# Measured durations as the interleaver's prices, streams that wait until an engine should be done, a chunked convolution and sums issued by need, in a streaming encoder layer on one core

## The chip, the cores and the metric

The kernel runs on one core of a Trainium2 chip. The metric is device time in microseconds (us) of one execution. TensorE (PE) multiplies matrices, VectorE (DVE), ScalarE (ACT) and GpSimd (POOL) work on tiles of 128 partitions, SyncE (SP) and POOL issue DMA transfers. Each engine takes its instructions in the order in which the program lists them for that engine, and an instruction waits on semaphores for what it reads or overwrites.

## The reference

One inference step of one layer on 512 prompt tokens and 8 sequences of 16 sample tokens (640 tokens, 1024 channels). Three branches come out of one projection, are gated and summed, and a feed-forward part follows. All in float32.

```python
z = x @ w_in                                   # 1024 -> 6656
xa, ya, glu, q, gates = split(z)
h = rg_lru(causal_depthwise_conv(xa, width 4))  # associative scan over positions
out_a = (h * gelu(ya)) @ proj_a
u = glu[..., :512] * sigmoid(glu[..., 512:])
v = causal_depthwise_conv(concat(history 30, u), width 31)
out_b = silu(layer_norm(v)) @ proj_b
out_c = mem_cross_attention(q, k, v) @ proj_c   # 4 heads, 256 memory tokens
g = sigmoid(gates + b_gate)
merged = g0 * out_a + g1 * out_b + g2 * out_c
x = layer_norm(alpha * x + merged @ w_out)
x = layer_norm(alpha * x + (silu(x @ w_ffn_gate) * (x @ w_ffn_up)) @ w_ffn_down)
```

The outputs are x for both groups and the new states of the two convolutions, of the recurrence and of the memory's keys and values.

## The kernel before

**Precision and tiles.** A float32 matrix is written as a high and a low part in the matmul's fp32r type; a product takes three matmuls (high by high, high by low, low by high). The activations lie with channels on partitions and the 640 tokens along the free dimension, as `xh` and `xl` (eight blocks of 128 channels). A matmul takes a 128x128 weight block and 320 tokens. ACT copies a weight tile to its high part (`wh`), DVE, and for some steps POOL, subtracts it from the float32 tile to get the low part (`wl`). Other tiles come from a pool of 52 slots of 128x640 (`Slots`, L110), handed out in the order in which they were freed; `s` with a number is such a slot.

**The list of steps.** `Step` (L268) is one weight tile with its matmuls. The list holds, in order: the memory's keys and values, the GLU halves and the queries, the recurrence's input `xa`, the gate of branch c and `proj_c`, gate and `proj_b` in turns, the recurrence's gate `ya`, gate 0 with pairs of column blocks, `proj_a`, `w_out`, the feed-forward part, and the down projection in two passes. The loop at the end runs over the list: it prepares the high part of a coming step (`prep_hi`), the low part of this one (`prep_lo`), calls the step's `before`, and issues the matmuls; a step's evacuation (`evac`) is put into `pending` and issued at the next `flush`.

**Pairs.** From gate 0 on, two column blocks by two token halves of 320 are computed with seven products in place of eight (`seven`, L1464), a scheme like Strassen's: m1 to m7 are products of 4 weight blocks by 4 activation blocks, that is, of sums and differences of quarters. `Pair` forms those of the weights (t1 to t4), `sums_stream` (L1386) those of the activations (s1 to s4), once for gate 0 (`sums0`) and once for the feed-forward part (`sums1`). A sum takes DVE additions over 128x640, an ACT copy to the high part and a DVE subtraction for the low part; in `sums0` the split of s1 goes into `xh` and `xl` themselves, once these quarters are not needed in their old form. All of `sums0` or `sums1` is forced with `finish` before the second product of the first pair.

**Streams and the planner.** Work that is no weight step (attention, the depthwise convolution, its normalisation, the recurrence, the sums) is written as generators, called streams: `attn`, `b`, `lru`, `a`, `sums0` and others. After each group of matmuls `advance` (L325) goes through the streams and issues the next piece of each as long as the planner's time of DVE or of ACT is behind that of PE. `Engine` (L53) adds a price for each issued instruction to its engine's time; the prices are formulas of the tile's width (`price_vector` L75, `price_scalar` L89, `price_tensor` L101). A stream that yields None stops for this round of `advance`. POOL has no price and no time. `finish(name)` issues all that is left of a stream at once; it stands before `proj_c` (`attn`), before `proj_b` (`b`), before `proj_a` (`lru` and `a`) and before the first pairs' second product.

**The convolution of width 31** (`conv_b_taps`, L796, for each of four blocks k of 128 channels): one ACT instruction for the last tap with the bias, then for each of 30 taps two DVE instructions scalar_tensor_tensor, one over the prompt (511 down to 482 tokens) and one over the eight sample sequences (128), whose history of 30 lies in a slot `us[k]` of 8 chunks of 46. `ln_b_stream` (L850) then adds the four blocks on POOL, multiplies the sum by a matrix of ones on PE to get the mean over channels, and goes on with the squares; between POOL's addition and the matmul stands one `yield None`.

**Attention.** `attn_prompt` (L947) and `attn_sample` (L1058) alternate matmuls on PE into a PSUM tile `pv` with softmax pieces on ACT and DVE; between the pieces stands `yield None`.

**The recurrence.** `a_stream` (L1355) multiplies the recurrence's output by the gelu gate and splits the product into `aT`, for each of eight blocks: a DVE multiplication, an ACT copy, a DVE subtraction. `proj_a` reads `aT`.

**The down projection.** `before_down` (L1709) is called before its first step: it frees the sums, splits the first two of 22 blocks of the hidden layer (`split_h`, L1701) into high and low, and issues the loads of the residual. The blocks k + 2 are split in the step of block k.

Of the kernel before, what the change touches and what calls it, by code (L numbers as in the profile page):

```python
# [7 lines left out]
F32 = mybir.dt.float32  # L8
# [24 lines left out]
NSLOT = 52  # L33
# [41 lines left out]
def price_vector(e, name, a, k):  # L75
    if name in ("tensor_reduce", "bn_stats"):
        return 70 + elements(a[1]) / 0.96
    n = elements(a[0])
    if name == "tensor_tensor_scan":
        return 70 + 2 * n / 0.96  # L80
# [29 lines left out]
class Slots:  # L110
    def __init__(self, pool, n):
        self.pool = pool
        self.free_list = list(range(n))
        self.at = {}
        self.count = 0
        self.low = n

    def get(self, shape, dtype=F32):
        if not self.free_list:
            raise RuntimeError("no slot is free")  # L120
        i = self.free_list.pop(0)
        self.low = min(self.low, len(self.free_list))
        self.count += 1
        x = self.pool.tile([128, T], dtype, name=f"s{i}_{self.count}", tag=f"s{i}", bufs=1)
        x = view(x, shape)
        self.at[id(x)] = (i, x)
        return x

# [15 lines left out]
def trunk(ctx, tc, x_prompt, x_sample, mem_prompt, state_conv_a, state_lru, state_conv_b, cache_mem_k, cache_mem_v,  # L144
# [7 lines left out]
    G, S = nc.gpsimd, nc.sync  # L152
# [172 lines left out]
    def advance(few=False):  # L325

        for e in (V, A):
            e.time = max(e.time, state["since"])
        state["since"] = P.time
        for item in list(streams):  # L330
# [3 lines left out]
            while max(V.time, 0 if name in vector_next else A.time) < P.time:  # L334
# [9 lines left out]
                if c == "v":  # L344
                    vector_next.add(name)

# [276 lines left out]
    us = {}  # L623
# [19 lines left out]
    def param_stream():  # L643
# [15 lines left out]
        for k in range(KC):  # L659
            us[k] = get([128, NB, 46])  # L660
# [4 lines left out]
        for i in range(2):  # L665
            for k in range(KC):
                copy(us[k][:, 4 * i:4 * i + 4, 0:30],
# [92 lines left out]
    def glu_steps(i):  # L760
# [7 lines left out]
        for k in (2 * i, 2 * i + 1):  # L768
            def evac_a(p, k=k):
                u = sg.pop(k)  # L770
                each(V.tensor_mul, u, two(u), p)
                copy(us[k][:, :, 30:46], u[:, TP:].rearrange("p (b t) -> p b t", t=TS))
                up[k] = u
# [22 lines left out]
    def conv_b_taps(k):  # L796
        v = get([128, T])
        vb[k] = v
        u, h = up[k], us[k]
        vs = v[:, TP:].rearrange("p (b t) -> p b t", t=TS)  # L800
        w = lambda j: pb[:, k, j:j + 1]
        A.activation(v, u, AF.Identity, scale=w(30), bias=pb[:, k, 31:32])
        yield "v"
        for j in range(29, -1, -1):
            s = 30 - j
            V.scalar_tensor_tensor(v[:, s:TP], u[:, :TP - s], w(j), v[:, s:TP], op0=OP.mult, op1=OP.add)
            V.scalar_tensor_tensor(vs, h[:, :, j:j + 16], w(j), vs, op0=OP.mult, op1=OP.add)
            yield "v" if j else 1

    def conv_b_stream():  # L810
        for k in range(KC):
# [3 lines left out]
            free(us[k])  # L815
            if k == 1:
# [3 lines left out]
                free(up[0], up[1])  # L820
            elif k > 1:
                free(up[k])

    def conv_b_states():
        yield from room()
        p = pv()
        for k in range(KC):
            P.transpose(p[:, 0, k * 128:(k + 1) * 128], up[k][:, TP:], ident)
            P.transpose(p[:30, 1, k * 128:(k + 1) * 128], up[k][:, TP - 30:TP], ident)
# [20 lines left out]
    def ln_b_stream():  # L850
# [9 lines left out]
        yield None  # L860
# [18 lines left out]
        yield None  # L879
        yield None  # L880
# [12 lines left out]
        yield 1  # L893
# [1003 lines left out]
```

## Time and profile before

| | |
|---|---|
| median of 3 runs | 1102.43 us (1102.43 to 1102.51) |
| the profiled execution, its own time | 1102.82 us |
| its span, from the first to the last instruction | 1101.1 us |
| mean granted clock of TensorE | 0.989 |
| PE, 6827 matmuls | busy 1064.1 us, 97% |
| DVE, 1333 instructions | busy 799.0 us, 73% |
| ACT, 861 instructions | busy 486.9 us, 44% |
| POOL, 185 instructions | busy 165.0 us, 15% |

Times are of one profiled execution. A row of a group gives engine, operation, output and inputs by the program's names, shapes and count, then busy time, the mean of one in ns, and the idle time before them with what ended it. All operations that go through `Engine` have the line of its helper, L64, so that the tiles' names tell them apart: `pu` and `pv` are PSUM tiles, `wr` a loaded weight tile, `wh` and `wl` its parts, `s` any slot, `pb` the convolution's taps. A row of the timeline is a run of like instructions: start, length, engine, operation, count and, in brackets, the idle time of the engine ahead of it and what ended it. PEclk is the clock that the throttle granted to TensorE, as a share of the full one.

### The profile page before, as it was taken

The page shows a single profiled execution, that of the slowest core. Times are in us where ns is not written, and L with a number is a line of the kernel's source. Part 1 is how long each engine was busy: PE and PEld are TensorE (multiplying, and loading weights), DVE is VectorE, ACT ScalarE, POOL GpSimd, SP SyncE. Part 2 cuts the span into 40 slices and gives each one's busy share as a digit, 9 for nine tenths or more (in the row PEclk, how much of TensorE's full clock was granted, in tenths as well). Part 3 has the DMA queues.
Part 4 walks back from the last instruction along what each step waited for, and adds up shares of the span by engine and source line. Part 5 has one row for each costly group of instructions (what it writes and reads, how often), then busy time and mean ns, then how long its engine had stood idle before and what let it go on. Part 6 is the DMA issues. An engine that isn't in the chain of part 4 may idle for free.

```text
span 1101.1 us, 16991 instructions
## 1 busy us (share of the span) xinstructions
PE 1064.1 (97%) x6827; PEld 1007.0 (91%) x6827; DVE 799.0 (73%) x1333; ACT 486.9 (44%) x861; POOL 165.0 (15%) x185
## 2 busy tenths in 40 slices
PE   8799898998999999999999999999999999999997
PEld 6699898997999999999999889899999999788886
DVE  6929898994465865699655579888887887544775
ACT  4532545445648346646423023444444443344341
POOL 3623323556200000010001120000000000100111
PEclk9999999998999999999999999999999999999999
DMA  9732123353313113212325431222233222734481
GB/s 339 252 95 78 39 67 96 118 154 94 118 39 96 59 58 115 78 44 77 115 78 172 148 120 59 71 82 78 77 95 97 77 77 86 278 115 132 165 294 39
DMA packets 80334, 123.11 MB, mean 112 GB/s; under 512 B 4075, under 2 KB 59371, under 8 KB 80256
## 3 DMA queue, kind: packets, MB, share of 16 engines
q1 hardware_dynamic: 73168, 100.36, 27.6%
q0 software_dynamic: 7088, 21.68, 6.3%
q8 instruction: 53, 0.87, 0.3%
q14 instruction: 25, 0.20, 0.1%
HBM read 112.41 MB, written 9.61 MB: 111 GB/s over the span
## 4 chain that ended last, share of the span: by engine, by line
PE 76%; DVE 14%; ACT 3%; issue 2%; POOL 2%; DMA 1%; SPq 0%; DVEq 0%; ACTq 0%; POOLq 0%
PE pu L64 67%; DVE s L64 12%; PE pv L64 9%; ACT s L64 2%; DVE wl L64 1%; ACT L64 1%; POOL s L540 1%; POOL s L541 1%; DMA s<-in_w_mem_k 0%; ACT wh L64 0%; DMA wr<-in_w_ffn_down 0%; DMA s<-in_x_prompt 0%; DVE xres L64 0%; DVE xl L64 0%; DVE mx L64 0%
## 5 line engine op out<-in xcount | busy, mean ns | idle before, releaser
L64 PE MATMUL pu<-xh,wh 128*128 128x320 f32 x1040 | 251.7, 314 | 4.6 <-ACT s L64 3.0
L64 PE MATMUL pu<-xh,wl 128*128 128x320 f32 x1040 | 246.9, 310 | 0.0
L64 ACT ACTIVATE wh<-wr 128x1024 fp32r<-128x1024 f32 (+1 forms) x149 | 135.1, 908 | 236.8 <-PE pu L64 139.0
L64 PE MATMUL pu<-xl,wh 128*128 128x320 f32 x888 | 219.4, 310 | 0.0
L64 PE MATMUL pu<-s,wh 128*128 128x320 f32 x1064 | 185.7, 310 | 1.6 <-ACT s L64 1.1
L64 PEld LDWEIGHTS pu<-xh,wh 128*128 128x128 f32 x1040 | 177.6, 189 | 9.4 <-ACT s L64 3.8
L64 PEld LDWEIGHTS pu<-xh,wl 128*128 128x128 f32 x1040 | 177.5, 189 | 0.0
L64 DVE TENSOR_TENSOR s<-s,s 128x640 fp32r<-128x640 f32 (+4 forms) x176 | 124.1, 723 | 62.4 <-ACT s L64 57.2
L64 PEld LDWEIGHTS pu<-s,wh 128*128 128x128 f32 x1064 | 163.4, 188 | 3.0 <-ACT s L64 1.7
L64 DVE TENSOR_TENSOR wl<-wr,wh 128x1024 fp32r<-128x1024 f32 (+1 forms) x100 | 114.1, 1142 | 67.6 <-ACT wh L64 67.6
L64 PEld LDWEIGHTS pu<-xl,wh 128*128 128x128 f32 x888 | 154.0, 189 | 0.6 <-DVE xl L64 0.6
L64 PE MATMUL pu<-s,wl 128*128 128x320 f32 x808 | 148.6, 311 | 2.8 <-ACT s L64 1.6
L64 DVE TENSOR_TENSOR s<-s,pu 128x320 f32<-128x320 f32 x186 | 87.8, 484 | 79.9 <-PE pu L64 77.1
L64 DVE SCALAR_TENSOR_TENSOR s<-s,pb,s 128x511 f32<-128x511 f32 (+14 forms) x240 | 130.1, 614 | 7.8 <-ACT s L64 7.8
L64 PEld LDWEIGHTS pu<-s,wl 128*128 128x128 f32 x808 | 126.6, 189 | 3.8 <-DVE s L64 1.9
L64 ACT ACTIVATE s<-s 128x640 fp32r<-128x640 f32 (+4 forms) x144 | 86.9, 628 | 97.2 <-DVE s L64 94.7
L64 PE MATMUL pu<-wh,s 128*128 128x512 f32 (+1 forms) x396 | 117.6, 390 | 3.0 <-ACT s L64 2.6
L64 PEld LDWEIGHTS pu<-wh,s 128*128 128x128 f32 x396 | 73.8, 191 | 18.2 <-ACT s L64 2.9
L64 ACT ACTIVATE s<-pu 128x320 f32<-128x320 f32 (+2 forms) x90 | 36.7, 442 | 75.5 <-PE pu L64 75.5
L64 PE MATMUL pu<-wl,s 128*128 128x512 f32 (+1 forms) x198 | 63.3, 391 | 1.5 <-POOL wl L305 0.8
L305 POOL TENSOR_TENSOR wl<-wr,wh 128x1024 fp32r<-128x1024 f32 x13 | 44.4, 3414 | 83.1 <-ACT wh L64 70.3
L64 PE MATMUL pv<-wh,s 128*128 128x512 f32 (+1 forms) x152 | 48.7, 368 | 0.4 <-DVE xres L64 0.4
(139 smaller groups left out, 1241.6 us busy)
## 6 DMA issues: line engine op xcount, KB each, us to landing
wr<-in_w_in SPq DMA_DIRECT2D x26, 1024.0 KB, 5.2
wr<-in_w_ffn_down SPq DMA_DIRECT2D x19, 1024.0 KB, 5.0
wr<-in_w_ffn_gate SPq DMA_DIRECT2D x11, 1024.0 KB, 5.4
wr<-in_w_ffn_up SPq DMA_DIRECT2D x11, 1024.0 KB, 5.4
s<-in_cache_mem_k POOLq DMA_DIRECT2D x16, 256.0 KB, 7.4
s<-in_cache_mem_v POOLq DMA_DIRECT2D x16, 256.0 KB, 6.9
wr<-in_proj_a SPq DMA_DIRECT2D x4, 1024.0 KB
wr<-in_w_out SPq DMA_DIRECT2D x4, 1024.0 KB, 5.9
```

The source lines that it names most:

```text
L64: return f(*a, **k)
L305: self.eng.tensor_tensor(l, x, f32(h), op=OP.subtract)
L540: G.tensor_tensor(y[1], y[1], g[1], op=OP.mult)
L541: G.tensor_tensor(y[1], y[1], b[1], op=OP.add)
```

## The change

It has five parts. (1) *Prices.* The formulas get larger constants, and POOL gets a price and a time like DVE and ACT. (2) *Waits of streams.* `settle(*engines)` yields until PE's planned time has reached that of the given engines, and stands at eight places, at seven of them where a `yield None` stood. (3) *The convolution* reads a tile of its own for each k, `u{k}`, in which the 512 prompt tokens and the 128 sample tokens lie as 40 chunks of 16 with their 30 earlier tokens (46 wide), so that a tap is one instruction over 640. ACT copies the history from chunk to chunk. The four tiles (three slots wide each) take the place of 12 slots and are handed out as 12 parts (`m`) for splits once their taps are issued. (4) *Sums by need.* `sums_stream` forms s2 and s3 first, then s1, then s4; `sum_there(n)` forces a sum just before the product that reads it; the first pair runs its products in the order m1, m4, m2, m6, m7, m5, m3. (5) *The first two splits of the hidden layer* go from `before_down` to the `before` of two late products of the last pair.

```diff
-NSLOT = 52
+NSLOT = 40
...
     if name in ("tensor_reduce", "bn_stats"):
-        return 70 + elements(a[1]) / 0.96
+        return 110 + elements(a[1]) / 0.96
...
-    return (130 if name == "scalar_tensor_tensor" else 70) + n / 0.96
+    return (230 if name == "scalar_tensor_tensor" else 146) + n / 0.951
+
+def price_pool(e, name, a, k):
+    if name == "dma_start":
+        return 600
+    return 150 + 3.2 * elements(a[0])
...
-    t = 130 + elements(a[0]) / 1.2
+    t = 180 + elements(a[0]) / 1.164
...
     if a[1].dtype == F32R:
-        return n / 2.4 + 2.5
+        return n / 2.4 + 13.3
...
-    G, S = nc.gpsimd, nc.sync
+    G, S = Engine(nc.gpsimd, price_pool), nc.sync
...
-        for e in (V, A):
+        for e in (V, A, G):
             e.time = max(e.time, state["since"])
...
+    def settle(*engines):
+        t = max(e.time for e in engines or (V, A))
+        yield None
+        while P.time < t:
+            yield None
...
+                u = us[k]
+                for c in range(2):
+                    V.tensor_mul(u[:, 20 * c:20 * c + 20, 30:46],
+                                 *(y.rearrange("p (c n) -> p c n", n=TS) for y in (c2(sg[k])[:, c], p[c])))
+                free(sg.pop(k))
+                copy(u[:, 1:32, 14:30], u[:, 0:31, 30:46])
+                copy(u[:, 2:32, 0:14], u[:, 0:30, 32:46])
...
         for j in range(29, -1, -1):
-            s = 30 - j
-            V.scalar_tensor_tensor(v[:, s:TP], u[:, :TP - s], w(j), v[:, s:TP], op0=OP.mult, op1=OP.add)
-            V.scalar_tensor_tensor(vs, h[:, :, j:j + 16], w(j), vs, op0=OP.mult, op1=OP.add)
+            V.scalar_tensor_tensor(v3, h[:, :, j:j + 16], w(j), v3, op0=OP.mult, op1=OP.add)
...
         y = total(vb)
         yield 1
-        yield None
+        yield from settle(G)
...
+        yield from part("s2", "11", True)
+        yield from part("s3", "21")
+        if in_place is None:
+            yield from part("s1", "22")
+        for i in blocks:
+            whole("12", i)
+            yield "v"
+            mix("12", "12", "11", i)
+            free(a.pop(("11", i)))
+            yield "v"
+        yield from part("s4", "12")
...
-            if i == 1:
-                before = begin
+            if first and xn[0] == "s":
+                before = lambda xn=xn: sum_there(xn)
...
+    for k in range(2):
+        assert steps[-5 + k].before is None
+        steps[-5 + k].before = lambda k=k: split_h(k)
...
     def before_down():
         sums_over()
-        for k in range(2):
-            split_h(k)
```

Three places show how the order on an engine moves. In these rows a slot bears its number and a running number.

On DVE, the end of gate 0 and the start of `proj_a`. `s<-s,pu` is the evacuation of a product, `wl<-wr` the low part of a weight tile. Before, these rows stand around the evacuations of the last pair; the last row of stream `a`, which subtracts the high part of a tile of `aT`, stands first.

```order
L64 TENSOR_TENSOR s_343_5644<-s_262_4493,s_342_5643 128x640
L64 TENSOR_TENSOR wh<-s_334_5532,wh 128x512
L64 TENSOR_TENSOR s_344_5665<-s_344_5665,pu 128x320
L64 TENSOR_TENSOR wl<-s_336_5552,wl 128x512
L64 TENSOR_TENSOR wh<-s_337_5554,wh 128x512
L64 TENSOR_TENSOR s_345_5666<-s_344_5665,pu 128x320
L64 TENSOR_TENSOR wl<-wr,wl 128x512
L64 TENSOR_TENSOR s_347_5737<-s_345_5666,pu 128x320
L64 TENSOR_TENSOR wl<-wr,wh 128x1024
L64 TENSOR_TENSOR s_346_5699<-s_345_5666,pu 128x320
L64 TENSOR_TENSOR wl<-wr,wh 128x1024
L64 TENSOR_TENSOR s_347_5737<-s_344_5665,pu 128x320
```

In the changed kernel the evacuation of the last product (`s_336`) is followed by these rows.

```order
L64 TENSOR_TENSOR s_336_5580<-s_329_5498,pu 128x320
L64 TENSOR_TENSOR s_335_5578<-s_223_3637,s_334_5577 128x640
L64 TENSOR_TENSOR s_244_4244<-s_244_4244,s_287_4842 128x640
L64 TENSOR_TENSOR m_2195<-s_244_4244,m_2195 128x640
L64 TENSOR_TENSOR s_250_4331<-s_250_4331,s_296_4914 128x640
L64 TENSOR_TENSOR m_2539<-s_250_4331,m_1722 128x640
L64 TENSOR_TENSOR s_256_4421<-s_256_4421,s_297_4983 128x640
L64 TENSOR_TENSOR m_2539<-s_256_4421,m_2539 128x640
L64 TENSOR_TENSOR s_262_4571<-s_262_4571,s_298_5031 128x640
L64 TENSOR_TENSOR m_2195<-s_262_4571,m_1164 128x640
L64 TENSOR_TENSOR wl<-wr,wh 128x1024
```

Nine 128x640 rows of stream `a`, the last subtraction of one tile and the multiplications and subtractions of four, have moved from ahead of the last pair's evacuations to behind all of them.

On DVE, the first pair of the feed-forward part. Before, after the evacuation of a product of the first steps, all mixes and splits of the sums' second half stand together ahead of the pair's second product.

```order
L64 TENSOR_TENSOR s_407_6923<-s_407_6923,pu 128x320 x2
L64 TENSOR_TENSOR wh<-wr,wh 128x512
L64 TENSOR_TENSOR s_418_7014<-s_416_6983,s_418_7014 128x640
L64 TENSOR_TENSOR s_416_6983<-s_419_7027,s_416_6983 128x640
L64 TENSOR_TENSOR s_417_7012<-s_417_7012,s_416_6983 128x640
L64 TENSOR_TENSOR s_423_7046<-s_416_6983,s_422_7045 128x640
L64 TENSOR_TENSOR s_425_7050<-s_418_7014,s_424_7049 128x640
L64 TENSOR_TENSOR s_427_7054<-s_419_7027,s_426_7053 128x640
L64 TENSOR_TENSOR s_429_7058<-s_417_7012,s_428_7057 128x640
```

In the changed kernel s1 and s4 stand between the evacuations of the pair's fifth, sixth and seventh product; `m_2195` is the low part of s1's second block, `s_426` and `s_428` are s4's two blocks.

```order
L64 TENSOR_TENSOR s_416_6882<-s_415_6881,pu 128x320
L64 TENSOR_TENSOR s_421_6914<-s_416_6882,pu 128x320
L64 TENSOR_TENSOR m_2195<-s_398_6724,m_2195 128x640
L64 TENSOR_TENSOR s_426_6957<-xh,xl 128x640
L64 TENSOR_TENSOR wl<-wr,wl 128x512
L64 TENSOR_TENSOR s_427_6975<-s_416_6882,pu 128x320
L64 TENSOR_TENSOR s_426_6957<-s_426_6957,s_397_6693 128x640
L64 TENSOR_TENSOR s_428_6979<-xh,xl 128x640
L64 TENSOR_TENSOR s_428_6979<-s_428_6979,s_406_6813 128x640
L64 TENSOR_TENSOR s_430_6983<-s_426_6957,s_429_6982 128x640
L64 TENSOR_TENSOR s_432_6987<-s_428_6979,s_431_6986 128x640
```

The splits that were done before the second product now lie behind evacuations of later products of the same pair.

On ACT, the end of the last pair and the start of the down projection. `wh<-wr 128x1024` is the high part of a row of the down weights, `s<-s 128x640` the high part of a hidden block. Before:

```order
L64 ACTIVATE wl<-s_585_9500 128x512
L64 ACTIVATE wh<-s_586_9502 128x512
L64 ACTIVATE wl<-wr 128x512
L64 ACTIVATE wh<-wr 128x1024 x3
L64 ACTIVATE s_594_9709<-s_402_6882 128x640
L64 ACTIVATE s_596_9713<-s_407_6923 128x640
L64 ACTIVATE s_598_9726<-s_434_7109 128x640
```

In the changed kernel:

```order
L64 ACTIVATE wl<-s_582_9332 128x512
L64 ACTIVATE s_588_9445<-s_400_6728 128x640
L64 ACTIVATE wh<-s_583_9334 128x512
L64 ACTIVATE s_590_9465<-s_405_6768 128x640
L64 ACTIVATE wl<-wr 128x512
L64 ACTIVATE wh<-wr 128x1024 x3
L64 ACTIVATE m_1722<-s_421_6914 128x640
```

The copies of the first two hidden blocks have moved from behind the three rows of down weights to ahead of them.

More of the change, by code (lines that the diff above doesn't have):

```diff
@@ L127, in get, with add @@
         return x
+    def add(self, tile):
+        for k in range(tile.shape[1] // T):
+            self.parts[len(self.parts)] = tile[:, k * T:(k + 1) * T]
+            self.free_list.append(("part", len(self.parts) - 1))
     def free(self, *xs):
@@ L893, in ln_b_stream @@
         yield 1
+        yield from settle(G)
         yield from room()
@@ L1134, in attn_sample @@
         yield 1
+        yield from settle()
         yield from room()
@@ L1155, in attn_sample @@
         yield 1
+        yield from settle()
         yield from room()
```

163 lines of the change are left out of this document (98 added, 65 removed).

## The prediction

> **What bounds the kernel now.** I read the page first, then the waits of TensorE, then a table by stages, then single places.
>
> ```profile
> span 1101.1 us, 16991 instructions
> PE 1064.1 (97%) x6827; PEld 1007.0 (91%) x6827; DVE 799.0 (73%) x1333; ACT 486.9 (44%) x861; POOL 165.0 (15%) x185
> PE 76%; DVE 14%; ACT 3%; issue 2%; POOL 2%; DMA 1%; SPq 0%; DVEq 0%; ACTq 0%; POOLq 0%
> ```
>
> TensorE (PE) is busy 1064.1 of 1101.1 us. The change leaves its work alone, so it can only win back the 37 us in which PE stands still, some of them at the start and the end of the kernel, and the time in which its clock is halved.
>
> ```profile
> engine line waited for: us in total, times, longest us
> PE pu L64 <- ACT s L64: 8.3, 5, 2.6
> PE pv L64 <- POOL s L855: 5.0, 1, 5.0
> ```
> ```profile
> core 0: us, PE busy (x) PEld busy (x) DVE busy (x) ACT busy (x) POOL busy (x), PEclk, DMA share, GB/s
> 100.00:240.00 140.00, 132.72 (x950) 128.28 (x949) 130.01 (x252) 70.62 (x176) 53.99 (x61) 0.99 0.31 93
> 240.00:260.00 20.00, 14.99 (x95) 12.93 (x93) 17.77 (x31) 8.37 (x18) 10.30 (x12) 0.83 0.35 105
> 260.00:320.00 60.00, 58.90 (x499) 56.36 (x498) 25.92 (x54) 34.53 (x59) 18.03 (x16) 1.00 0.29 92
> 320.00:480.00 160.00, 158.39 (x1070) 156.51 (x1070) 105.73 (x171) 94.27 (x144) 5.62 (x10) 1.00 0.24 76
> 480.00:500.00 20.00, 19.32 (x132) 19.06 (x131) 17.84 (x27) 9.95 (x19) 0.00 (x0) 1.00 0.09 31
> 680.00:700.00 20.00, 17.91 (x109) 17.16 (x108) 19.38 (x32) 6.96 (x13) 0.00 (x0) 0.91 0.00 1
> 930.00:950.00 20.00, 17.37 (x89) 15.33 (x88) 12.64 (x19) 5.91 (x8) 3.68 (x7) 0.91 0.73 273
> ```
>
> Each stretch loses what it lacks of busy PE, and its length times what the granted clock lacks of 1. The attention and convolution stretch 100 to 240 lost 7.3 + 1.4 us, 240 to 260 lost 5.0 + 3.4, 260 to 320 lost 1.1, 320 to 480 lost 1.6; the first gate-0 pair (480 to 500) 0.7, the first FFN pair (680 to 700) 2.1 + 1.8, the start of the down projection (930 to 950) 2.6 + 1.8. VectorE (DVE) is full only in some of these: 130.0 of 140 us in the first.
>
> **The change part by part.** *The normalisation behind the convolution.*
>
> ```profile
> 252.11 1.53 POOL L855 TENSOR_TENSOR s<-s,s 128x640 f32<-128x640 f32 x1 [8.11 <-DVE s L64]
> ```
> ```profile
> 253.69 2.50 PE L64 MATMUL pv<-s,ones 128*128 128x512 f32 x4 [5.01 <-POOL s L855]
> ```
>
> The matmul with ones waits for GpSimd (POOL) to add the last convolved tile, and POOL had waited for the last tap. DVE is late against the order of the program. The change prices DVE, ACT and POOL, and holds the matmul until POOL should be done. Whether it is done depends on the taps:
>
> ```profile
> L64 DVE SCALAR_TENSOR_TENSOR s<-s,pb,s 128x511 f32<-128x511 f32 (+14 forms) x240 | 130.1, 614 | 7.8 <-ACT s L64 7.8
> ```
> ```profile
> L64 DVE SCALAR_TENSOR_TENSOR s<-s,pb,s 128x128 f32<-128x128 f32 x120 | 44.4, 370 | 0.0
> L64 DVE SCALAR_TENSOR_TENSOR s<-s,s 128x640 f32<-128x640 f32 x8 | 6.6, 820 | 1.8 <-ACT s L64 1.8
> L64 DVE SCALAR_TENSOR_TENSOR s<-s,pb,s 128x508 f32<-128x508 f32 x4 | 5.9, 1480 | 0.0
> L64 DVE SCALAR_TENSOR_TENSOR s<-s,pb,s 128x507 f32<-128x507 f32 x4 | 2.9, 736 | 0.0
> ```
>
> A tap is now a pair, a wide and a 128-wide instruction: 130.1/120 = 1.08 us on average, 0.74 + 0.37 = 1.11 where nothing disturbs it (the two overlap a little in the average), and more where it does, as in the 508 row. One 640-wide tap is not in the trace. From below it is the 820 ns of the same operation on plain tiles; from above 0.74 + 0.37 = 1.11, no gain. I take 0.85, nearest to the first row, since the strided 128-wide taps already read such chunks. 120 taps then take 102 instead of 130.1 us: up to 28 us off DVE, bounds 0 to 32. The added ACT copies (two of 31 and 30 chunks for each of four tiles, under the 0.73 us each that a 640-wide copy takes in a row below) lie on an engine with 70.6 busy of 140 and are costed at nothing; without that cover they would be up to 5.8 us. So DVE should be ahead of the plan, and I count 7.4 of the 8.4 us of 240 to 260 as won (bounds 0 and 8.4).
>
> *The attention waits.* The steps of attention now yield until both DVE and ACT should be done, where a single yield stood. A yield on this planner only holds back the stream's next piece; queued behind a PE instruction that waits are all later projection matmuls, so a held piece costs nothing as long as projections are left to issue, and they are (the stretch to 480 is 99% PE). Of the 7.3 + 1.4 + 1.1 us of 100 to 240 and 260 to 320 I take 7 as won (bounds 0 and 9.8), and 0.9 of the 1.6 us of 320 to 480.
>
> *The split ahead of the down projection.*
>
> ```profile
> 938.72 1.06 ACT L64 ACTIVATE wh<-wr 128x1024 fp32r<-128x1024 f32 x1 [5.08 <-DMA wr<-in_w_ffn_down]
> 939.68 1.98 ACT L64 ACTIVATE s<-s 128x640 fp32r<-128x640 f32 x3
> ```
> ```profile
> 940.45 1.22 PE L64 MATMUL pu<-wh,s 128*128 128x512 f32 x2 [2.63 <-ACT s L64]
> ```
>
> ACT stands 5.08 us for a load of weights that the first product doesn't need, and only then come the two copies that it needs. The change issues these two copies and their subtractions some steps earlier, past that wait. Next late would be the weights of the first row, which were split before 938. I count 2.6 + 1.8 = 4.4 as won (bounds 2 and 4.4). Won in all: 7.4 + 7 + 0.9 + 4.4 = 19.7.
>
> *What is issued late now.* These are the durations for the three places that lose.
>
> ```profile
> 696.05 236.51 PE pu L64 x1608
> ```
> ```profile
> L64 DVE TENSOR_TENSOR s<-s,pu 128x320 f32<-128x320 f32 x186 | 87.8, 484 | 79.9 <-PE pu L64 77.1 <-ACT wl L64 0.4
> L64 DVE TENSOR_TENSOR s<-s,s 128x640 fp32r<-128x640 f32 x64 | 51.5, 821 | 50.9 <-ACT s L64 47.8 <-issue 3.1
> ```
> ```profile
> L64 ACT ACTIVATE s<-s 128x640 fp32r<-128x640 f32 x64 | 45.5, 731 | 49.0 <-DVE s L64 46.5 <-issue 2.5
> L64 ACT ACTIVATE s<-pu,pa 128x320 f32<-128x320 f32 x36 | 17.1, 521 | 5.8 <-PE pu L64 5.7
> ```
>
> A 128x320 matmul takes 236.51/1608 = 0.147 us, a product of twelve 1.76 us, and a row of proj_a's six 0.88 us.
>
> (l) *proj_a.* The higher prices let stream "a" fall behind. By the order of after, four tiles of it stand behind the evacuation of the last gate-0 product: for each a multiply (0.82), a copy on ACT (0.73) and a subtraction (0.82), one after the other, some 2.5 us with the hand-overs. Ahead of them stand an evacuation and a subtraction, 0.48 + 0.82. The eighth tile is there 1.3 + 4 x 2.5 = 11.3 us after the last product, and PE wants it after 7 x 0.88 = 6.2. Stall 5.1 us less what the products' own pipeline gives, 4.5, and one stretch of half clock, 1.7: 6 (bounds 3 and 8).
>
> (m) *First gate-0 pair.* The in-place split of s1 stands behind the evacuations of the product ahead: 0.48 + 0.41 on DVE, 0.52 on ACT, then copy 0.73 and subtraction 0.82, with hand-overs 3.3 us, and 1.7 of half clock. 0.7 was lost before and 0.4 of the stall is the product's own work: 3.9 more (bounds 1 and 6).
>
> (g) *First FFN pair.* s1 waits for an evacuation (0.48), a copy (0.73, partly beside it) and a subtraction (0.82): 2.2 us. s4, one product later, for an evacuation, two sums and two mixes of which three must be over (3 x 0.82), a copy and a subtraction: 4 us more. With 1.9 of half clock 8.1; before it lost 2.1 + 1.8 = 3.9: 4.2 more (bounds -4 and 6, since the first needs of s2 and s3 are met sooner than the full set was).
>
> Lost in all: 6 + 3.9 + 4.2 = 14.1. The rest I cost at nothing: 40 slots (and twelve parts after the taps) are handed out longest-free first, so what a new tile waits for was let go many operations before; one late release would cost about one tile operation, 0.8. Eight small memsets lie on POOL, which is busy 15% of the span; at the 0.37 us of the smallest tap row they would be 3 us uncovered.
>
> The half clock is a term of its own here:
>
> ```profile
> 690.66 0.42 PE L64 MATMUL pu<-s,wl 128*128 128x320 f32 x1 [1.60 <-ACT s L64]
> ```
> ```profile
> 690.00:694.00 4.00, 2.90 (x10) 2.67 (x11) 4.00 (x6) 3.53 (x6) 0.00 (x0) 0.66 0.00 0
> ```
>
> After an idle time of 1.60 us, and with another small one behind it, the granted clock is 0.66 over 4 us. The Trainium skill ("TensorE: Matmul & The Clock Gate", Part 1) says that the clock falls to half only after a whole idle window of about 3.4 us. By that rule the three new stalls would lose no clock: lost 8.8 instead of 14.1, and the sum below would be 1091.9. The trace differs from the page in this, and I go by the trace.
>
> Sum: 1102.8 (the profiled execution; span 1101.1 and 1.7 around it) - 19.7 + 14.1 = 1097.2. The median of the runs, 1102.4, lies 0.4 below that execution, so I forecast **1097.0**. By the bounds of the terms that I doubt most it may be 1092 to 1101.
>
> **The rivals.** *DVE runs well ahead of its prices* (A): 1087, chance 0.25.
>
> ```profile
> 688.16 5.51 DVE L64 TENSOR_TENSOR s<-s,s 128x640 f32<-128x640 f32 x7
> ```
>
> Seven 640-wide operations take 0.79 us each back to back, where the new price is 0.82. If "a" and the sums have no more than their last link open at the three places, these cost 5 instead of 14.1: 1102.4 - 19.7 + 5 = 1087.7, rounded down for 0.9 us at other small waits. Against it: the order fixes that those links stand behind an evacuation, however fast DVE is.
>
> *The waits only move* (B): 1102, chance 0.17. The planner's clock is not the chip's: `settle` holds by added prices, and POOL's disturbance of DVE has no price. If the taps stay late and the matmul with ones still waits, 5.4 us of the gain are gone: 1097.0 + 5.4 = 1102.4.
>
> *The forced rests decide* (C): 1110, chance 0.08. The chain DVE, ACT, DVE behind the last evacuation costs its upper bounds, 8 + 6 + 6, plus 3.4 us of clock at proj_a where four short stalls follow each other, 23.4 in all, and only 15.7 are won: 1102.4 + 7.7. It decides from losses above 19.7.
>
> *POOL beside wide taps* (D): 1118, chance 0.05.
>
> ```profile
> L305 POOL TENSOR_TENSOR wl<-wr,wh 128x1024 fp32r<-128x1024 f32 x13 | 44.4, 3414 | 83.1 <-ACT wh L64 70.3 <-DVE s L64 7.4 <-PE pv L64 5.5
> ```
>
> One in four 508-wide taps must have taken 4 x 1480 - 3 x 736 = 3.7 us, 3 us over the others. If each of the 13 splits held up a wide tap so, 39 us would be lost: 102 + 39 is 11 us more than the taps take now, and DVE has 10 idle between 100 and 240. Then the gains of the stretches up to 480 go (15.3), and the down projection's 4.4 stands against 14.1 and 6 of late evacuations (a second stall like l): 1102.4 - 4.4 + 14.1 + 6 = 1118. It decides from a tap of about 1.1 us on average. The Trainium skill ("GPSIMD Engine Reference", quick table) says that GpSimd shares its SBUF interfaces with VectorE, in contention with DVE instructions that read two inputs from SBUF; the 508 row agrees, but the number of POOL's operations doesn't change.
>
> **How the numbers follow.** Forecast 0.45, A 0.25, B 0.17, C 0.08, D 0.05. The range takes in A and B with their bounds: 1086 to 1106; it leaves out C and D, 0.13. About 0.2% (2.2 us) is what a measurement of this kernel tells from no change: faster 0.70 (forecast and A), same 0.17 (B), slower 0.13 (C and D).
>
> **What would show it.** Right: no wait of PE for POOL at the ones matmul; 120 taps with a mean near 850 ns; no wait at the first matmul of the down projection; new waits of PE for DVE or ACT at proj_a's first rows and in the first pairs, each with a dip of the granted clock. Wrong: DVE still above 90% between 100 and 240, a tap near 1.1 us, or proj_a without a stall.

## The result, and the profile after

The changed kernel takes 1120.7 us (median of four runs, 1119.2 to 1122.15), against 1102.43: the ratio is 1.0167, with a 95% interval of 1.0154 to 1.0179. It is slower by 18.3 us. I had forecast 1097.0 with a range of 1086 to 1106, so neither the direction nor the range held.

The page of the changed kernel's profile, first the span, then the busy times, then the chain that ended last:

```profile
span 1117.4 us, 16897 instructions
PE 1070.0 (96%) x6827; PEld 1009.6 (90%) x6827; DVE 793.8 (71%) x1213; ACT 501.7 (45%) x879; POOL 161.2 (14%) x193
PE 66%; DVE 15%; ACT 6%; issue 4%; DMA 1%; POOL 1%; DVEq 0%; ACTq 0%; POOLq 0%
```

PE has the same 6827 matmuls. It idles 47.4 us (1117.4 - 1070.0) where it idled 37.0, and its busy time is 5.9 us longer with a granted clock of 0.985 in place of 0.989 (0.004 of the span is 4.5 us). DVE has 120 instructions fewer and is busy only 5 us less. What PE waited for:

```profile
engine line waited for: us in total, times, longest us
PE pv L64 <- POOL s L64: 10.4, 5, 6.6
PE pu L64 <- DVE s L64: 8.8, 10, 2.7
PE pu L64 <- ACT s L64: 4.0, 3, 2.1
```

The wait for POOL, whose end the change meant to see ahead, has not gone: its longest piece is 6.6 us and was 5.0. The table by stages, with the same columns as before (length, busy times, granted clock, DMA). The first row is of the kernel before, the others are of the changed kernel:

```profile
60.00:100.00 40.00, 40.00 (x273) 39.39 (x273) 23.44 (x44) 12.72 (x29) 9.33 (x3) 1.00 0.26 81
```
```profile
60.00:100.00 40.00, 37.33 (x243) 36.24 (x242) 21.85 (x25) 14.54 (x34) 6.05 (x4) 0.97 0.26 82
...
100.00:240.00 140.00, 135.66 (x981) 131.57 (x980) 129.43 (x164) 71.49 (x182) 55.02 (x62) 1.00 0.31 93
240.00:260.00 20.00, 13.41 (x87) 11.69 (x87) 13.32 (x19) 10.96 (x21) 13.72 (x13) 0.83 0.34 105
260.00:320.00 60.00, 59.46 (x506) 57.40 (x505) 23.07 (x46) 28.60 (x48) 13.91 (x14) 1.00 0.31 97
320.00:500.00 180.00, 176.14 (x1185) 173.69 (x1184) 118.50 (x189) 113.61 (x164) 1.49 (x2) 1.00 0.22 68
500.00:520.00 20.00, 16.14 (x95) 15.03 (x95) 12.77 (x22) 9.14 (x18) 0.00 (x0) 0.91 0.17 53
...
540.00:580.00 40.00, 36.85 (x219) 34.40 (x218) 27.20 (x38) 16.12 (x24) 3.49 (x7) 0.91 0.27 83
...
700.00:740.00 40.00, 34.23 (x211) 32.90 (x210) 31.71 (x54) 15.51 (x30) 0.00 (x0) 0.91 0.17 53
...
930.00:960.00 30.00, 30.00 (x203) 29.74 (x202) 23.90 (x42) 12.13 (x22) 2.00 (x4) 1.00 0.35 117
```

With each stretch's loss counted as in the prediction (idle PE, and its length times what the clock lacks of 1), the account is:

| stretch | lost before | lost after |
|---|---|---|
| 60 to 260, convolution and attention | 17.1 | 18.2 |
| 260 to 320 | 1.1 | 0.5 |
| 320 to the first gate-0 pair, and that pair | 2.3 | 3.9 + 5.7 |
| start of `proj_a` | 0 | 6.8 |
| first FFN pair | 3.9 | 9.4 |
| start of the down projection | 4.4 | 0 |

The sum of the differences is 15.7 us; the spans differ by 16.3. The first line of the table hides three moves: from 100 to 240 PE loses 4.3 us where it lost 8.7, but 3.9 us are lost between 60 and 100, where nothing was lost before, and from 240 to 260 it loses 10.0 where it lost 8.4. So the places that I had costed as losses lose about what I said or a little more, the down projection wins what I said, and the 15 us that the convolution, the attention and the recurrence should have won are not there.

### The profile page after: what moved, and what is told of

It reads as the page before. It is cut to its first block, busy times and chain, and to the rows that moved or that the text cites. A ratio compares the mean times of both kernels' runs of the same rounds, so it can differ in the third digit from the quotient of the medians.

```text
span 1117.4 us, 16897 instructions
## 1 busy us (share of the span) xinstructions
PE 1070.0 (96%) x6827; PEld 1009.6 (90%) x6827; DVE 793.8 (71%) x1213; ACT 501.7 (45%) x879; POOL 161.2 (14%) x193
## 4 chain that ended last, share of the span: by engine, by line
PE 66%; DVE 15%; ACT 6%; issue 4%; DMA 1%; POOL 1%; DVEq 0%; ACTq 0%; POOLq 0%
PE pu L64 59%; DVE s L64 12%; PE pv L64 8%; ACT s L64 3%; ACT L64 2%; DVE wl L64 1%; ACT wh L64 1%; DVE m L64 1%; ACT m L64 1%; DMA wr<-in_proj_a 0%; DVE xres L64 0%; POOL wl L64 0%; POOL s L64 0%; DMA out<-s 0%; POOL out L64 0%
## 5 line engine op out<-in xcount | busy, mean ns | idle before, releaser
L64 PE MATMUL pu<-m,wh 128*128 128x320 f32 x700 | 124.6, 313 | 7.3 <-DVE s L64 4.0
L64 DVE SCALAR_TENSOR_TENSOR s<-u,pb,s 128x640 f32<-128x640 f32 x120 | 120.8, 1008 | 10.4 <-ACT s L64 4.5
L64 DVE TENSOR_TENSOR s<-s,s 128x640 f32<-128x640 f32 (+4 forms) x132 | 92.8, 711 | 41.4 <-ACT s L64 39.2
L64 PEld LDWEIGHTS pu<-m,wh 128*128 128x128 f32 x700 | 107.5, 189 | 12.0 <-DVE s L64 3.0
L64 PE MATMUL pu<-m,wl 128*128 128x320 f32 x564 | 101.3, 311 | 2.1 <-ACT m L64 1.6
L64 PEld LDWEIGHTS pu<-m,wl 128*128 128x128 f32 x564 | 87.6, 189 | 2.8 <-ACT m L64 1.9
L64 PE MATMUL pu<-wh,s 128*128 128x512 f32 (+1 forms) x292 | 86.1, 389 | 0.3 <-ACT wh L64 0.3
L64 PE MATMUL pu<-s,wh 128*128 128x320 f32 x376 | 71.5, 318 | 3.0 <-ACT s L64 2.1
L64 PEld LDWEIGHTS pu<-s,wh 128*128 128x128 f32 x376 | 61.0, 196 | 3.6 <-ACT s L64 2.3
L64 DVE TENSOR_TENSOR m<-s,m 128x640 fp32r<-128x640 f32 (+1 forms) x41 | 31.5, 789 | 30.9 <-ACT m L64 30.8
```

The source lines that it names most:

```text
L64: return f(*a, **k)
```

## The experiments

Theory 1, formed after reading this: the wide tap is no faster than the pair of taps that it replaces, `settle` waits by a planner's clock that runs ahead of DVE, the higher prices make the streams late for `proj_a`, and the sums by need put chains between products. The rivals stand with each run. Times are medians, beside runs of the kernel before of 1102.2 to 1102.5 us on the same chips; each kernel has four runs or ten. The changed kernel was not run again beside them, so differences from its 1120.7 us are across chips.

**The chunked convolution alone**, on the kernel before: `conv_b_taps` with its tiles, 40 slots and the twelve parts.

```diff
-            V.scalar_tensor_tensor(v[:, s:TP], u[:, :TP - s], w(j), v[:, s:TP], op0=OP.mult, op1=OP.add)
-            V.scalar_tensor_tensor(vs, h[:, :, j:j + 16], w(j), vs, op0=OP.mult, op1=OP.add)
+            V.scalar_tensor_tensor(v3, h[:, :, j:j + 16], w(j), v3, op0=OP.mult, op1=OP.add)
```

> The kernel before with the chunked convolution alone (its tiles, 40 slots and twelve parts, one 640-wide tap). Theory 1 (a wide tap, 0.92 us from start to start in the changed kernel, is no faster than the pair of narrow taps, 0.895): 1102.4 +- 3, the taps with a mean near 1.0 us, DVE over 125 of the 140 us from 100 to 240, and the matmul with ones still waiting 4 to 7 us for POOL. Rival (the wide tap does free DVE, and the new prices and waits spoil it): 1090 to 1096, and that wait under 1 us.

Measured: 1106.9 us, ratio 1.0048 (1.0030 to 1.0066). So this kernel is 4.6 us slower than the one before beside it (1102.25); that is a little outside the 3 us that I gave theory 1, and far from the rival. The old price formula stayed: by it a wide tap costs 0.80 us and the pair in its place 0.90 to 0.93, so the planner counts the convolution as cheaper than it was, and what of the 4.6 us is due to this was not tested. The group of taps, and the matmul with ones in the timeline:

```profile
L64 DVE SCALAR_TENSOR_TENSOR s<-u,pb,s 128x640 f32<-128x640 f32 x120 | 121.5, 1014 | 10.5 <-ACT s L64 4.5 <-issue 2.3
```
```profile
251.60 1.12 PE L64 MATMUL pv<-s,ones 128*128 128x512 f32 x1 [3.65 <-POOL s L876]
```

The mean is 1.01 us, and the wait is 3.65 us, a little under the 4 to 7 that I expected. DVE is busy 124.5 us of 100 to 240 where I expected over 125. Why so little is won is seen in runs of undisturbed taps. The first two rows are from the timeline of the kernel before, where two instructions are a tap; the last two are from the changed kernel:

```profile
80.79 3.78 DVE L64 SCALAR_TENSOR_TENSOR s<-s,pb,s 128x511 f32<-128x511 f32 x8 [1.19 <-ACT s L64]
151.38 4.60 DVE L64 SCALAR_TENSOR_TENSOR s<-s,pb,s 128x494 f32<-128x494 f32 x10
```
```profile
81.90 3.65 DVE L64 SCALAR_TENSOR_TENSOR s<-u,pb,s 128x640 f32<-128x640 f32 x4 [2.33 <-issue]
95.75 6.46 DVE L64 SCALAR_TENSOR_TENSOR s<-u,pb,s 128x640 f32<-128x640 f32 x7
```

Four taps took 3.78 us as eight narrow instructions and take 3.65 us as four wide ones, 0.03 us a tap. These were the widest pairs; further on five pairs took 4.60 us and seven wide taps take 6.46, 0.92 us a tap in both. Over the undisturbed taps of the whole convolution the time from the start of a tap to that of the next instruction is 0.91 us for a pair and 0.90 for a wide tap, so that 120 taps gain 1 us. The durations of the pair (0.75 and 0.37) sum to 1.12, but back to back they overlap.

What is lost shows between 80 and 100. There PE lost nothing before, and here it idles 2.8 us and loses 1.8 more at a clock of 0.91. Six taps in a row stand ahead of the evacuation that PE needs, first in the kernel before, then in this one, then PE's wait here:

```profile
85.62 5.59 DVE L64 SCALAR_TENSOR_TENSOR s<-s,pb,s 128x507 f32<-128x507 f32 x12
```
```profile
86.61 7.63 DVE L64 SCALAR_TENSOR_TENSOR s<-u,pb,s 128x640 f32<-128x640 f32 x6
```
```profile
94.70 1.03 PE L64 MATMUL pu<-xh,wh 128*128 128x320 f32 x2 [2.81 <-DVE s L64]
```

A split of weights runs on POOL in both. The six pairs took no more than undisturbed ones, while one of the six wide taps was stopped for 2.0 us. The changed kernel has the same wait (2.67 us).

**The two hidden-layer splits alone**, on the kernel before.

```diff
+    for k in range(2):
+        assert steps[-5 + k].before is None
+        steps[-5 + k].before = lambda k=k: split_h(k)
...
-        for k in range(2):
-            split_h(k)
```

> The kernel before with the first two hidden-layer splits moved ahead, and nothing else. Theory 1 (this term stands by itself): 1098.0, 4.4 us less than before, and no wait at the first matmul of the down projection. Rival (the first weights are late next): 1101 to 1102.4, with a wait of PE for ACT wh there.

Measured: 1097.01 us, ratio 0.9957 (0.9942 to 0.9972). The stretch around the start of the down projection has lost its wait and its half clock:

```profile
925.00:955.00 30.00, 30.00 (x162) 26.82 (x161) 18.68 (x26) 14.43 (x20) 3.68 (x7) 1.00 0.65 234
```

PE is busy all 30 us at full clock. This term was right, and it is the one part of the change that pays.

**The changed kernel with the old prices** (of DVE, ACT and PE; POOL keeps its own).

```diff
-    return (230 if name == "scalar_tensor_tensor" else 146) + n / 0.951
+    return (130 if name == "scalar_tensor_tensor" else 70) + n / 0.96
...
-    t = 180 + elements(a[0]) / 1.164
+    t = 130 + elements(a[0]) / 1.2
...
-        return n / 2.4 + 13.3
+        return n / 2.4 + 2.5
```

> The changed kernel with the old prices of DVE, ACT and PE (POOL keeps its price). Theory 1 (the higher prices make stream a late): the 8.2 us lost at the start of proj_a go, the pairs' starts get better by some 2 us, 1108 to 1112. Rival (the sums by need push stream a back, whatever the prices): 1118 or more, with proj_a's waits as they are.

Measured: 1110.44 us, 10.3 less than with the new prices (ratio to before 1.0074, 1.0055 to 1.0093). Its table at `proj_a` and at the first FFN pair:

```profile
540.00:580.00 40.00, 40.00 (x274) 40.00 (x274) 22.88 (x33) 15.19 (x21) 0.00 (x0) 1.00 0.32 106
700.00:740.00 40.00, 34.24 (x205) 32.76 (x204) 28.64 (x50) 14.74 (x28) 0.00 (x0) 0.87 0.20 59
```

`proj_a` starts without any wait: the prices are what held stream `a` back. The first FFN pair still loses 5.8 + 5.2 us, so that part of the loss is not the prices'.

**The changed kernel with the old sums**: four sums forced before the second product, products in the old order.

```diff
-            if first and xn[0] == "s":
-                before = lambda xn=xn: sum_there(xn)
+            if i == 1:
+                before = begin
```

> The changed kernel with the old sums: all four forced before the second product, products in the old order. Theory 1 (the chain behind each product's evacuation is what the two pair starts lose): their losses fall from 6.2 and 9.3 to about 0.9 and 4.3 as before the change, 1109 to 1112, and proj_a keeps its 8 us. Rival (the prices make DVE late at these places too): 1116 or more, with a long wait before the second product instead.

Measured: 1118.49 us, 2.2 less; theory 1 as I had put it misses, and its rival is right here. With the new prices the old sums are late too:

```profile
500.00:520.00 20.00, 17.78 (x111) 17.52 (x110) 15.57 (x27) 10.36 (x19) 0.00 (x0) 0.91 0.16 53
540.00:580.00 40.00, 37.34 (x201) 32.64 (x200) 28.64 (x40) 16.84 (x26) 4.12 (x8) 0.83 0.26 83
700.00:740.00 40.00, 35.76 (x241) 35.01 (x240) 35.64 (x61) 14.44 (x27) 0.00 (x0) 1.00 0.17 53
```

The first gate-0 pair loses 4.0 us and the FFN pair 4.2, less than with the sums by need (5.7 and 9.4), but `proj_a` loses 9.5 instead of 6.8. Its waiting did not grow (2.7 us, 3.2 with the sums by need); the difference is half clock.

**The changed kernel with the hold at the ones matmul made 8 us longer.**

```diff
-        yield from settle(G)
+        yield from settle(G, more=8000)
```

> The changed kernel with 8 us added to the time that the first matmul with ones is held for POOL. Theory 1 (the planner's clock runs some 7 us ahead of DVE there, because POOL's stalls of the taps have no price, so the hold ends too soon): the wait of 6.6 us falls under 1 and its half clock goes, 1110 to 1113. Rival (the wait moves on to the steps behind it): 1117 or more.

Measured: 1113.45 us, 7.3 less, half a microsecond short of the range that I gave theory 1. The stretch that lost the most, and the matmul with ones itself:

```profile
230.00:250.00 20.00, 20.00 (x155) 17.98 (x154) 17.25 (x20) 7.55 (x12) 3.78 (x2) 1.00 0.00 1
```
```profile
248.25 1.24 PE L64 MATMUL pv<-s,ones 128*128 128x512 f32 x4
```

No wait is left in front of it, and no half clock. So there was enough other work for PE, and `settle` had let go too early.

**No weight splits on POOL**, in the changed kernel and in the kernel before with the moved hidden-layer splits.

```diff
-                 eng=G if ld is loads[0] and o == 0 or 12 <= len(steps) < 36 and len(steps) % 2 else V)
+                 eng=G if ld is loads[0] and o == 0 else V)
```

> The changed kernel with the 12 weight splits that POOL does between the GLU and the xa steps done by DVE. Theory 1 (each of them stops a tap for 2 us, more than the 1.2 us that it costs on DVE itself, and DVE's price covers it there): no tap near 2.9 us, their mean at 0.89 to 0.93, the waits at 92.8 and at the matmul with ones under 2 us, 1107 to 1112. Rival (15 us more on a full DVE): 1118 or more, with new waits for evacuations.

> The kernel before with the moved hidden-layer splits (1097.0 alone) and the same 12 weight splits done by DVE. Theory 1: 1086 to 1091, the wait at the matmul with ones (4.9 us there) under 2. Rival (DVE fuller by 15 us): 1096 or more.

Measured: 1108.22 us (ratio 1.0050, 1.0035 to 1.0065), 12.5 less than the changed kernel, and 1094.24 us (0.9924, 0.9909 to 0.9939), 2.8 less than with the moved splits alone. The shortest, median and longest tap, in the changed kernel and then without POOL's splits:

```profile
L64 DVE SCALAR_TENSOR_TENSOR s<-u,pb,s x120: 853/885/2918, 81.9 to 245.1; 128x640 f32<-128x640 f32 x120
```
```profile
L64 DVE SCALAR_TENSOR_TENSOR s<-u,pb,s x120: 847/885/2085, 81.9 to 240.1; 128x640 f32<-128x640 f32 x120
```

With POOL splitting, the longest taps take 2.0 us over the median, and each of them runs beside an operation of POOL. Without it the taps' mean falls from 1008 to 903 ns, the last one starts 5 us earlier although DVE does 12 splits more, the wait of 2.67 us before 100 is 0.58, and PE waits half a microsecond at the matmul with ones:

```profile
243.59 1.35 PE L64 MATMUL pv<-s,ones 128*128 128x512 f32 x4 [0.52 <-POOL s L64]
```

On the older kernel the convolution's stretches are whole, too:

```profile
100.00:240.00 140.00, 140.00 (x1033) 136.82 (x1033) 132.91 (x275) 74.54 (x187) 37.72 (x59) 1.00 0.36 108
240.00:260.00 20.00, 19.84 (x181) 18.08 (x179) 11.98 (x21) 12.26 (x23) 12.83 (x14) 1.00 0.34 107
```

PE loses 0.2 us where it lost 17.1. But the time fell by 2.8 us, between the 6 to 11 that I expected and the 1 at most of the rival: the first gate-0 pair (480 to 500) loses 5.0 us and the stretch from 520 to 580 loses 5.7. My reading is that the splits now have a price on DVE and the planner issues the streams later; the run with cheaper prices below bears this out. The move does two things at once, and these runs don't part them: it takes the stalls away, and it makes the planner count 12 splits more on DVE. DVE itself is hardly freer: in the changed kernel it is busy 790.9 us without POOL's splits and 793.8 with them.

**settle alone**, on the kernel before with the moved hidden-layer splits: the eight waits, and POOL priced; the other prices are the old ones.

```diff
-    G, S = nc.gpsimd, nc.sync
+    G, S = Engine(nc.gpsimd, price_pool), nc.sync
...
-        yield None
+        yield from settle(G)
...
-            yield None
+            yield from settle()
```

> The kernel before with the moved hidden-layer splits and the waits of streams (settle, with POOL priced), old prices of the rest. Theory 1 (settle holds by the planner's clock, which is not late where DVE is): 1095 to 1098, the wait at the matmul with ones still 3 to 5 us. Rival (settle does win the attention's and POOL's waits, and only the prices spoil it): 1091 or less.

Of the eight places, not seven but four had a `yield None` before (one had two); at the other four, three of them in the attention, the hold is new, not put in place of one.

Measured: 1100.86 us (ten runs, 1099.23 to 1102.76; ratio 0.9986, 0.9977 to 0.9995), 3.8 more than without it. It lies above theory 1's range, and further from the rival. Nothing is won at the convolution, and something is lost at the first gate-0 pair:

```profile
240.00:260.00 20.00, 14.99 (x96) 12.92 (x95) 16.96 (x31) 8.85 (x19) 9.17 (x11) 0.91 0.35 105
480.00:500.00 20.00, 16.77 (x114) 15.89 (x112) 18.22 (x28) 13.22 (x27) 4.12 (x8) 1.00 0.04 8
```

The wait in the first row is 5.0 us as before the change; in the second PE idles 3.2 us where it idled 0.7.

**The sums by need alone**, on the kernel before with the moved hidden-layer splits, old prices.

```diff
-            if i == 1:
-                before = begin
+            if first and xn[0] == "s":
+                before = lambda xn=xn: sum_there(xn)
...
-        for i, (n, u, opens, xn, wn) in enumerate(PRODUCTS):
+        products = [PRODUCTS[i] for i in ((0, 5, 2, 1, 3, 4, 6) if first else range(7))]
+        for i, (n, u, opens, xn, wn) in enumerate(products):
```

> The kernel before with the moved hidden-layer splits (1097.0 alone) and the sums by need, old prices and nothing else. Theory 1 (a sum that is forced right before its product stands behind the evacuation of the product ahead, whatever the prices): the two pair starts lose 4 and 10 us as with the old prices in the changed kernel, where they lost 0.9 and 4.3, 1104 to 1107. Rival (the sums by need gain time by themselves, two products more for s2 and s3): 1097 or less.

Measured: 1105.11 us, 8.1 more than with the moved splits alone (ratio 1.0024, 1.0015 to 1.0033). The stretch of the first FFN pair:

```profile
680.00:720.00 40.00, 34.23 (x205) 32.76 (x204) 30.49 (x51) 16.10 (x29) 0.00 (x0) 0.87 0.11 34
```

It loses 5.8 + 5.2 us, where 3.9 were lost before. The first gate-0 pair loses 1.9 us and not the 4 that I expected. The order of products and the chains between them cost that, with every price and wait as it was.

**One forced set of sums before the fourth product, and cheaper prices of DVE.** All three stand on the kernel before with the moved hidden-layer splits and no weight splits on POOL. In the first and third kernel the first pair's products m7 and m3 begin to add into their accumulators ahead of the evacuations of m6 and m5, which read the same ones: the first pair's outputs are not the reference's there, and the wait that the right order would need is missing from their times.

```diff
-            if i == 1:
-                before = begin
+            if first and xn == "s2":
+                before = first
```
```diff
-    return (130 if name == "scalar_tensor_tensor" else 70) + n / 0.96
+    return (100 if name == "scalar_tensor_tensor" else 30) + n / 0.96
```

> The moved hidden-layer splits, DVE doing POOL's 12 weight splits (together 1094.2), and the first pair's products in the new order with all four sums of the old stream forced once, before the fourth product. Theory 1 (two products more before one forced chain, no chain between products): the pair starts fall from 5.0 and 4.3 to under 1.5 each, 1087 to 1090. Rival (the chain begins behind an evacuation all the same): 1093 or more.

> The moved hidden-layer splits, DVE doing POOL's 12 weight splits (1094.2), and the prices of DVE 40 ns (30 for scalar_tensor_tensor) under the old ones. Theory 1 (streams that the planner issues earlier aren't forced, and DVE can bear it once POOL doesn't stop it): the losses before the second product (5.0) and at proj_a (6.7) shrink to half, 1087 to 1091. Rival (DVE falls behind the plan from 100 to 260 again): 1095 or more, with a wait at the matmul with ones.

> The two kernels before this one together: one forced set of sums before the fourth product, and the lower prices of DVE. Theory 1: the gains add, 1082 to 1087. Rival (they take away the same loss): 1088 to 1091.

Measured: 1098.72, **1089.07** and 1090.88 us (ratios 0.9968, 0.9954 to 0.9981; 0.9878, 0.9861 to 0.9896; 0.9894, 0.9878 to 0.9910). The new order doesn't pay even without that wait, so that the rival is right for the first kernel, and the third gains nothing by it. The cheaper prices give 5.2 us. That kernel, the second, beats both: 13.4 us under the kernel before, 31.6 under the changed one. Theory 1 and its rival both show in its table:

```profile
240.00:260.00 20.00, 16.98 (x103) 15.11 (x96) 9.23 (x16) 12.52 (x25) 16.80 (x14) 0.83 0.42 120
320.00:500.00 180.00, 178.22 (x1204) 176.28 (x1204) 133.74 (x210) 109.57 (x170) 5.63 (x10) 1.00 0.22 71
500.00:580.00 80.00, 80.00 (x548) 80.00 (x547) 46.07 (x73) 31.50 (x51) 1.12 (x2) 1.00 0.30 97
```

Between 500 and 580, `proj_a` included, PE loses nothing any more; at 240 to 260 it loses 3.0 + 3.4 again, because DVE is behind such a plan. A price between the two was not tried.

## Why the prediction was wrong

*The cost of a tap* failed first: the step from 130.1 us of taps to 102, "up to 28 us off DVE". The changed kernel's taps are busy 120.8 us:

```profile
L64 DVE SCALAR_TENSOR_TENSOR s<-u,pb,s 128x640 f32<-128x640 f32 x120 | 120.8, 1008 | 10.4 <-ACT s L64 4.5 <-issue 2.3
```

My 0.85 us for a wide tap was near its median of 0.885. The error lay in the other side of the comparison. The 1.08 us that I had for a pair is an average with the taps that POOL stops in it; I read 1.11, the sum of the two durations, as the cost of an undisturbed pair, where the time from one to the next instruction is 0.91. So of the 0.23 us between 1.08 and 0.85 some 0.16 were stalls (nine pairs over 2 us had lost 19 us in all), which a wide tap doesn't take away: eight wide taps over 2 us still lose 15. And of the 9 us by which the taps' busy time fell, some 4 are gaps of 0.03 us that now stand between wide taps, where the narrow ones overlapped. DVE was as late as before.

*That settle holds* failed with it. The prediction had the matmul with ones won by 7.4 us and the attention by 7, because "DVE should be ahead of the plan". The hold ends when PE's planned time reaches POOL's planned time. That time is made of POOL's own prices; that POOL must first wait for the last tap, and how late DVE is, are not in it. The 8 us of extra hold won 7.3 us, which shows that the work to fill the gap was there and that the hold ended too soon. The mechanism was my rival B, "the waits only move". I priced it at 5.4 us, for one of the two waits; in the balance from 60 to 320 all 14.4 of both are gone, and `settle` alone cost 3.8.

*The losses* were right in mechanism, each with a size of its own. At `proj_a` I said 6 us and 6.8 were lost, but 3.2 of them were waiting, where I put 4.5, and 3.6 half clock, where I put 1.7: that the sum came so near is luck. PE's rows there show the chain as the order had it (a multiplication, a copy, a subtraction per tile):

```profile
558.19 0.56 PE L64 MATMUL pu<-m,wh 128*128 128x320 f32 x2 [0.65 <-ACT m L64]
559.05 0.56 PE L64 MATMUL pu<-m,wh 128*128 128x320 f32 x2 [0.30 <-DVE m L64]
...
560.55 0.56 PE L64 MATMUL pu<-m,wh 128*128 128x320 f32 x2 [0.65 <-ACT m L64]
561.41 0.90 PE L64 MATMUL pu<-m,wh 128*128 128x320 f32 x2 [0.30 <-DVE m L64]
```

PE waits in turn for the copy and for the subtraction of each tile, which come 2.36 us apart; I had said 2.5. At the first gate-0 pair I expected a loss of 3.9 us more; 5.7 us in all were lost against 0.7, which is 5.0 more. Its chain, in the timeline of DVE, then of ACT, then of PE:

```profile
504.45 1.01 DVE L64 TENSOR_TENSOR s<-s,pu 128x320 f32<-128x320 f32 x2 [1.57 <-PE pu L64]
```
```profile
505.49 0.56 ACT L64 ACTIVATE s<-s,pa 128x320 f32<-128x320 f32 x1 [3.67 <-DVE s L64]
505.96 1.34 ACT L64 ACTIVATE xh<-s 128x640 fp32r<-128x640 f32 x2
```
```profile
506.73 0.57 PE L64 MATMUL pu<-xh,wl 128*128 128x320 f32 x1 [2.32 <-ACT xh L64]
```

The two evacuations, the sigmoid and the copy stand in the line that the prediction named. At the first FFN pair I said 8.1 us and 9.4 were lost. Here too the waiting was less than I had added up, 5.8 us for 6.2 (of which the second stall, put at 4, has links that sum to 4.5), and the half clock more, 3.6 for 1.9. Of the two parts behind these losses, the prices account for `proj_a` (gone with the old ones) and the sums by need for the FFN pair (there with everything else as before). The loss of the first gate-0 pair has no single part behind it: it is 1.9 us with the sums by need alone, 3.2 with `settle` alone and 4.0 with all but the sums by need.

*The hidden-layer splits* were right: 4.4 us forecast, 5.2 measured alone.

So the forecast's own balance of 19.7 won against 14.1 lost became about 5 won against 21 lost. The single runs give much the same account: the chunks 4.6 us, the prices 10.3 (taken out of the changed kernel), `settle` 3.8 and the sums by need 8.1, less 5.2 for the moved splits, are 21.6 us against the 18.3 measured together, so that the parts nearly add up. Rival D, that POOL disturbs wide taps, had the kind of cost (2.0 us where a split stops a tap, I said 3) but not the change as a whole, since the disturbance was there before. In one place it did come true: before 100 a wide tap is stopped where the narrow ones were not, PE loses 3.9 us there, and without POOL's splits its wait falls from 2.67 to 0.58 us.

## What to carry to other kernels

A merged instruction is worth what the time from one start to the next becomes, not what the durations sum to: read a run of them back to back. A planner that waits "until an engine should be done" is only as good as its prices at the stretch with the least slack, and what disturbs that engine has to be in them, or out of the kernel: moving POOL's splits to DVE, where they have a price, won 12.5 us, the waits alone nothing. Higher prices also delay all later streams, so what is won at one wait has to be set against the forced work at the places that need those streams.

## What the runs showed of the hardware

In the changed kernel seven of the twelve 128x1024 subtractions on POOL held up one DVE operation by 2.0 to 2.2 us; beside the other five no DVE operation lost more than 0.4. On DVE itself such a subtraction takes 1.2 us. With all twelve on DVE, its instructions rise from 1213 to 1225 and its busy time falls from 793.8 us to 790.9, so that the offloading saved DVE nothing.

Short waits close together brought TensorE's clock down as one long wait does. In the rows of `proj_a` above no wait is over 0.65 us, yet the matmuls from 561.41 on are slow (0.90 us for a pair that took 0.56), and the stretch has a granted clock of 0.91. The same waits don't always do so. The first row is of the changed kernel, the second is of the one with the longer hold, and both have the wait of 2.32 us for ACT at the first gate-0 pair:

```profile
495.00:520.00 25.00, 21.03 (x127) 19.66 (x126) 17.67 (x31) 12.71 (x26) 0.00 (x0) 0.93 0.14 43
```
```profile
490.00:515.00 25.00, 20.87 (x134) 19.48 (x133) 17.98 (x29) 12.07 (x23) 0.00 (x0) 1.00 0.13 43
```

The clock was 0.93 in one and 1.00 in the other. The Trainium skill ("TensorE: Matmul & The Clock Gate", Part 1) says that the window over which the activity is watched runs free of the kernel; two outcomes for the same waits agree with that, while its rule that only an idle window of some 3.4 us brings the clock down does not agree with these rows or those of the prediction. That the 3 us between the changed kernel's runs come from this was not shown.
